# RMSNorm with repeated rows: row sums, roots and copies spread anew over the engines

## The chip, the cores and the metric

One core of a Trainium2 chip. The metric is the device time of one execution in microseconds, median over several.

## The reference

```python
def reference(x, gamma):                      # x: 8 x 512 x 2048, gamma: 2048, float32
    x_rep = np.repeat(x, 2, axis=1)
    rms = np.sqrt((x_rep ** 2).mean(axis=-1, keepdims=True) + 1e-6)
    return ((x_rep / rms) * gamma[None, None, :]).astype(np.float32)
```

Each row of x is divided by its root mean square, multiplied by gamma, and written twice: 33.6 MB are read and 67.1 MB written.

## The kernel before

The rows go through in eight tiles of 128 partitions by four rows, in three buffers of eight rows each. A load fills the upper four rows. The results are put in every second row and copied to the rows between, and one 8 MB store takes the whole buffer. All loads and stores are issued by SyncE into one queue.

```python
    def square(i, k):                          # ScalarE: one row's sum of squares, then its root
        sq = junk.tile([P, D], f32, name="sq")
        ss = small.tile([P, 1], f32, name="ss")
        nc.scalar.activation(out=sq[:], in_=ys[i][:, K * (R - 1) + k, :], func=Act.Square, accum_out=ss[:])
        rms = small.tile([P, 1], f32, name="rms")
        nc.scalar.activation(out=rms[:], in_=ss[:], func=Act.Sqrt, scale=inv_d, bias=eps_t[:])
        return rms

    def scale(i, k, rms):                      # VectorE: x * (1 / rms) * gamma, one row
        rstd = small.tile([P, 1], f32, name="rstd")
        nc.vector.reciprocal(out=rstd[:], in_=rms[:])
        nc.vector.scalar_tensor_tensor(...)

    def compute(i):
        for k in range(K):
            scale(i, k, square(i, k))
        repeat(i, 0, K // 2, nc.scalar.copy)
        repeat(i, K // 2, K, nc.vector.tensor_copy)

    load(0, nc.sync, parts=2)
    # ... seven pieces of gamma by ScalarE's queue into one partition ...
    nc.gpsimd.partition_broadcast(out_ap=gamma_b[:], in_ap=gamma_b[0:1, :])
    # ...
    loads_after = {2: (3, 4, 5), 4: (6, 7)}
    for i in range(ntiles):
        compute(i)
        store(i, 0, K)
        for j in loads_after.get(i, ()):
            load(j, nc.sync)
```

Of the kernel before, what the change touches and what calls it, by code (L numbers as in the profile page):

```python
# [1 line left out]

# [4 lines left out]


@with_exitstack
def kernel(  # L10
    ctx: ExitStack,
    tc: tile.TileContext,
    x: bass.AP,
    gamma: bass.AP,
    out: bass.AP,
):
    nc = tc.nc
    P = nc.NUM_PARTITIONS
    f32 = mybir.dt.float32
    Act = mybir.ActivationFunctionType  # L20
    Alu = mybir.AluOpType

    B, S, D = x.shape
    Bo, So, Do = out.shape
    R = So // S
    assert R == 2 and D == Do and B == Bo and So == S * R
    eps = 1e-6
    inv_d = 1.0 / float(D)


    K = 4
    N = B * S
    assert N % (P * K) == 0
    ntiles = N // (P * K)
    x_t = x.rearrange("b s d -> (b s) d").rearrange("(n p k) d -> n p k d", p=P, k=K)
    out_t = out.rearrange("b s d -> (b s) d").rearrange("(n p j) d -> n p (j d)", p=P, j=K * R)

    singles = ctx.enter_context(tc.tile_pool(name="singles", bufs=1))
    rows = ctx.enter_context(tc.tile_pool(name="rows", bufs=3))
    junk = ctx.enter_context(tc.tile_pool(name="junk", bufs=1, space=bass.MemoryType.PSUM))  # L40
    small = ctx.enter_context(tc.tile_pool(name="small", bufs=8))

    ys = []

    def load(i, eng, parts=1):


        y = rows.tile([P, K * R, D], f32, name="y")
        step = K // parts
        for k in range(0, K, step):  # L50
            at = K * (R - 1) + k
            eng.dma_start(out=y[:, at : at + step, :], in_=x_t[i, :, k : k + step, :])
        ys.append(y)

    def store(i, k0, k1):
        nc.sync.dma_start(  # L56
            out=out_t[i, :, R * k0 * D : R * k1 * D],
            in_=ys[i][:, R * k0 : R * k1, :].rearrange("p j d -> p (j d)"),
        )

    def square(i, k):
        sq = junk.tile([P, D], f32, name="sq")
        ss = small.tile([P, 1], f32, name="ss")
        nc.scalar.activation(  # L64
            out=sq[:], in_=ys[i][:, K * (R - 1) + k, :], func=Act.Square, accum_out=ss[:]
        )
        rms = small.tile([P, 1], f32, name="rms")
        nc.scalar.activation(out=rms[:], in_=ss[:], func=Act.Sqrt, scale=inv_d, bias=eps_t[:])  # L68
        return rms

    def scale(i, k, rms):
        rstd = small.tile([P, 1], f32, name="rstd")
        nc.vector.reciprocal(out=rstd[:], in_=rms[:])  # L73
        nc.vector.scalar_tensor_tensor(  # L74
            out=ys[i][:, R * k, :], in0=ys[i][:, K * (R - 1) + k, :], scalar=rstd[:], in1=gamma_b[:],
            op0=Alu.mult, op1=Alu.mult,
        )

    def repeat(i, k0, k1, copy):
        y_r = ys[i].rearrange("p (k r) d -> p k r d", r=R)  # L80
        copy(out=y_r[:, k0:k1, 1, :], in_=y_r[:, k0:k1, 0, :])  # L81

    def compute(i):
        for k in range(K):
            scale(i, k, square(i, k))
        repeat(i, 0, K // 2, nc.scalar.copy)
        repeat(i, K // 2, K, nc.vector.tensor_copy)


    ctx.enter_context(tc.manual_schedule())  # L90
    load(0, nc.sync, parts=2)
    gamma_b = singles.tile([P, D], f32, name="gamma_b")
    cuts = [0, *range(D // 4, D + 1, D // 8)]
    for c0, c1 in zip(cuts, cuts[1:]):
        nc.scalar.dma_start(out=gamma_b[0:1, c0:c1], in_=gamma[c0:c1].partition_broadcast(1))  # L95
    nc.gpsimd.partition_broadcast(out_ap=gamma_b[:], in_ap=gamma_b[0:1, :])  # L96
    eps_t = singles.tile([P, 1], f32, name="eps_t")
    nc.vector.memset(eps_t, eps)  # L98
    load(1, nc.sync)
    load(2, nc.sync)  # L100



    assert ntiles == 8
    loads_after = {2: (3, 4, 5), 4: (6, 7)}
    for i in range(ntiles):
        compute(i)
        store(i, 0, K)
        for j in loads_after.get(i, ()):
            load(j, nc.sync)  # L110


# [1 line left out]
_INS = ['x', 'gamma']  # L114
_OUTS = [((8, 1024, 2048), 'float32')]


# [23 lines left out]
```

## Time and profile before

| | before |
|---|---|
| time, median of 6 runs | 239.77 us (239.54 to 240.25) |
| span of the profiled run | 237.9 us |
| VectorE / ScalarE / GpSimd busy | 41% / 42% / 1% |
| share of the sync queue's packets | 98.5% of sixteen engines |

The time is some 2 us over the span (239.77 against 237.9). The prediction shows the lines that carry the bound. Two more groups of this kernel's page show what the change set out to remove. The columns are line, engine, operation, tiles and count, then busy us and mean ns, then the engine's idle time just before and what ended most of it. The third line is the only work that GpSimd does here, but for four fills of constants at the start (0.1 us each).

```profile
L73 DVE RECIPROCAL rstd<-rms 128x1 f32<-128x1 f32 x32 | 5.0, 158 | 94.6 <-ACT rms L68 94.3
...
L68 ACT ACTIVATE rms<-ss,eps_t 128x1 f32<-128x1 f32 x32 | 9.4, 295 | 1.0
...
L96 POOL PARTITION_BROADCAST gamma_b<-gamma_b x1 | 2.3, 2294 | 12.2 <-DMA y<-in_x_dram 12.2
```

Each row has a root on ScalarE and a reciprocal on VectorE, 32 of each, and VectorE's idle time is put down to the root. It idles mostly because the data isn't there yet (ScalarE, which makes the roots, itself waits 87.8 us for loads), not because a root takes 295 ns.

### The profile page before, as it was taken

To read this page: it belongs to the slowest core of one execution; us is meant where nothing else is said; L and a number is where in the kernel's file an instruction comes from. 1 tells how busy PE (TensorE), PEld (TensorE's weight loads), DVE (VectorE), ACT (ScalarE), POOL (GpSimd) and SP (SyncE) were. 2 spreads that over 40 slices of the span, in tenths; PEclk is the share of its full clock that TensorE was granted. 3 is DMA by queue.
4 is the path that set the end of the run, shared out by engine and by line. 5 is a ranking of instruction groups with operands and counts; after the bars stand their busy time and mean duration, and the time that the engine had idled before them with its cause. 6 is when DMAs were issued, how large, how long until landed. Compare 5 with 4: busy or idle time off the path is not lost.

```text
span 237.9 us, 287 instructions
## 1 busy us (share of the span) xinstructions
DVE 96.5 (41%) x73; ACT 101.0 (42%) x106; POOL 2.5 (1%) x5
## 2 busy tenths in 40 slices
DVE  0049999960000000059999960000199990000000
ACT  2697999900000000099999920000599960000000
POOL 0030000000000000000000000000000000000000
DMA  7999998989899998999998999989998989999994
GB/s 265 436 446 441 441 441 353 530 353 496 386 452 430 397 485 353 441 441 441 441 518 364 464 419 430 452 369 430 435 518 364 518 364 485 397 452 430 408 474 176
DMA packets 2464, 100.69 MB, mean 423 GB/s; under 512 B 279, under 2 KB 285, under 8 KB 286
## 3 DMA queue, kind: packets, MB, share of 16 engines
q1 hardware_dynamic: 2448, 100.66, 98.5%
q14 instruction: 2, 0.02, 0.0%
q10 hardware_dynamic: 14, 0.01, 0.0%
HBM read 33.56 MB, written 67.11 MB: 423 GB/s over the span
## 4 chain that ended last, share of the span: by engine, by line
DMA 58%; ACT 12%; DVE 9%; issue 1%; POOLq 1%; ACTq 1%; SPq 0%
DMA y<-in_x_dram 33%; DMA out_dram<-y 21%; ACT sq L64 8%; DVE y L74 7%; DMA gamma_b<-in_gamma_dram 4%; ACT y L81 3%; DVE y L81 2%; ACT rms L68 1%; POOLq L136 1%; ACTq L95 1%; DVE rstd L73 0%; POOLq L96 0%; SPq L56 0%
## 5 line engine op out<-in xcount | busy, mean ns | idle before, releaser
L64 ACT ACTIVATE sq<-y 128x2048 f32<-128x2048 f32 x32 | 59.7, 1865 | 87.8 <-DMA y<-in_x_dram 87.8
L74 DVE SCALAR_TENSOR_TENSOR y<-y,rstd,gamma_b 128x2048 f32<-128x2048 f32 x32 | 75.3, 2352 | 4.1 <-POOL gamma_b L96 3.0
L73 DVE RECIPROCAL rstd<-rms 128x1 f32<-128x1 f32 x32 | 5.0, 158 | 94.6 <-ACT rms L68 94.3
L81 ACT COPY y<-y 128x4096 f32<-128x4096 f32 x8 | 28.7, 3590 | 1.4 <-DVE y L74 1.4
L81 DVE COPY y<-y 128x4096 f32<-128x4096 f32 x8 | 18.3, 2294 | 0.3
L68 ACT ACTIVATE rms<-ss,eps_t 128x1 f32<-128x1 f32 x32 | 9.4, 295 | 1.0
L64 ACT ACTIVATION_READ_ACCUMULATOR sq<-y 128x1 f32 x32 | 6.0, 187 | 0.0
L64 ACT ACT_TABLE_LOAD x1 | 1.3, 1283 | 3.0 <-issue 3.0
L96 POOL PARTITION_BROADCAST gamma_b<-gamma_b x1 | 2.3, 2294 | 12.2 <-DMA y<-in_x_dram 12.2
L68 ACT ACT_TABLE_LOAD x1 | 1.3, 1283 | 0.0
L98 DVE MEMSET eps_t<- 128x1 f32 x1 | 0.1, 59 | 0.8 <-PEq L125 0.8
L125 POOL MEMSET const-uint8-127<- 128x1 uint8 x1 | 0.1, 102 | 0.0
L125 POOL MEMSET const-bfloat16-1.0<- 128x1 bf16 x1 | 0.1, 101 | 0.0
L125 POOL MEMSET const-float32-0.0<- 128x1 f32 x1 | 0.1, 98 | 0.2 <-issue 0.2
L125 POOL MEMSET const-float32-1.0<- 128x1 f32 x1 | 0.1, 98 | 0.0
## 6 DMA issues: line engine op xcount, KB each, us to landing
y<-in_x_dram SPq DMA_DIRECT2D x7, 4096.0 KB, 14.6
y<-in_x_dram SPq DMA_DIRECT2D x2, 2048.0 KB, 7.4
out_dram<-y SPq DMA_DIRECT2D x8, 24.4
gamma_b<-in_gamma_dram ACTq DMA_DIRECT2D x6, 1.0 KB
gamma_b<-in_gamma_dram ACTq DMA_DIRECT2D x1, 2.0 KB
```

The lines of the kernel that those rows point to most:

```text
L64: nc.scalar.activation(out=sq[:], in_=ys[i][:, K * (R - 1) + k, :], func=Act.Square, accum_out=ss[:])
L68: nc.scalar.activation(out=rms[:], in_=ss[:], func=Act.Sqrt, scale=inv_d, bias=eps_t[:])
L73: nc.vector.reciprocal(out=rstd[:], in_=rms[:])
L74: nc.vector.scalar_tensor_tensor(out=ys[i][:, R * k, :], in0=ys[i][:, K * (R - 1) + k, :], scalar=rstd[:], in1=gamma_b[:], op0=Alu.mult, o ...
L81: copy(out=y_r[:, k0:k1, 1, :], in_=y_r[:, k0:k1, 0, :])
L95: nc.scalar.dma_start(out=gamma_b[0:1, c0:c1], in_=gamma[c0:c1].partition_broadcast(1))
L96: nc.gpsimd.partition_broadcast(out_ap=gamma_b[:], in_ap=gamma_b[0:1, :])
L98: nc.vector.memset(eps_t, eps)
L125: nc = _bacc.Bacc("TRN2", target_bir_lowering=False, num_devices=1)
L136: with _tile.TileContext(nc) as tc:
```

## The change

Its intent: fewer and wider instructions, with each engine's work ordered so that none waits for another. Row sums are made of wide squares (ScalarE) and wide sums (VectorE), roots as a power -0.5 on GpSimd for a whole tile, tile 5's copy on GpSimd, and a tile's squares ahead of the former tile's copies. Gamma's pieces go into the sync queue. Cut to its core:

```diff
-    def square(i, k):
-        # ... one row: square with sum, then sqrt, both on ScalarE
+    def square(i, k0, k1):
+        nc.scalar.activation(
+            out=ys[i][:, k0:k1, :], in_=ys[i][:, x_at + k0 : x_at + k1, :], func=Act.Square
+        )
+    def reduce(i, k0, k1, ss):
+        nc.vector.tensor_reduce(
+            out=ss[:, k0:k1], in_=ys[i][:, k0:k1, :], op=Alu.add, axis=mybir.AxisListType.X
+        )
+    def root(k0, k1, ss):
+        at = ss[:, k0:k1]
+        nc.gpsimd.tensor_scalar(
+            out=at, in0=at, scalar1=inv_d, scalar2=eps, op0=Alu.mult, op1=Alu.add
+        )
+        nc.gpsimd.tensor_tensor(out=at, in0=at, in1=power_t[:, k0:k1], op=Alu.pow)
 # ... cut: gamma's pieces go to the sync queue, into two half rows ...
-    nc.gpsimd.partition_broadcast(out_ap=gamma_b[:], in_ap=gamma_b[0:1, :])
+    for c0 in (0, D // 2):
+        nc.gpsimd.partition_broadcast(out_ap=gamma_b[:, c0 : c0 + D // 2], in_ap=gamma_half(c0))
 # ... cut: by_rows() and mixed() order the parts of one tile ...
-    for i in range(ntiles):
-        compute(i)
-        store(i, 0, K)
+    by_rows(0, whole)
+    two = mixed(sums(1, 1), shared, ahead=(2, 1))
+    mixed(two, shared)
 # ... cut: loads 3, 4, 5 ...
+    by_rows(3, shared)
+    _, _, ss = mixed(sums(4, H), whole, ahead=(5, 0))
 # ... cut: loads 6, 7 ...
+    reduce(5, 0, K, ss)
+    root(0, K, ss)
+    # ... tile 5: four ScalarE copies with a scale, one VectorE multiply of 8192 by gamma ...
+    repeat(5, 0, K, nc.gpsimd.tensor_copy)
+    store(5)
+    last = mixed(sums(6, 1), by_scalar, ahead=(7, 0))
+    mixed(last, shared)
```

More of the change, by code (lines that the diff above doesn't have):

```diff
@@ L43, with new_tile, load @@
     ys = []
-    def load(i, eng, parts=1):
-        y = rows.tile([P, K * R, D], f32, name="y")
-        step = K // parts
-        for k in range(0, K, step):
-            at = K * (R - 1) + k
-            eng.dma_start(out=y[:, at : at + step, :], in_=x_t[i, :, k : k + step, :])
-        ys.append(y)
-    def store(i, k0, k1):
+    def new_tile():
+        ys.append(rows.tile([P, K * R, D], f32, name="y"))
+    def load(i, k0, k1):
         nc.sync.dma_start(
-            out=out_t[i, :, R * k0 * D : R * k1 * D],
-            in_=ys[i][:, R * k0 : R * k1, :].rearrange("p j d -> p (j d)"),
-        )
@@ L61, in square, with store, total @@
-    def square(i, k):
+            out=ys[i][:, K * (R - 1) + k0 : K * (R - 1) + k1, :], in_=x_t[i, :, k0:k1, :]
+        )
+    def store(i):
+        nc.sync.dma_start(out=out_t[i], in_=ys[i].rearrange("p j d -> p (j d)"))
+    H = K // 2
+    x_at = K * (R - 1)
+    def total(i, k, ss):
         sq = junk.tile([P, D], f32, name="sq")
-        ss = small.tile([P, 1], f32, name="ss")
         nc.scalar.activation(
-            out=sq[:], in_=ys[i][:, K * (R - 1) + k, :], func=Act.Square, accum_out=ss[:]
+            out=sq[:], in_=ys[i][:, x_at + k, :], func=Act.Square, accum_out=ss[:, k : k + 1]
@@ L66, in square @@
         )
-        rms = small.tile([P, 1], f32, name="rms")
-        nc.scalar.activation(out=rms[:], in_=ss[:], func=Act.Sqrt, scale=inv_d, bias=eps_t[:])
-        return rms
-    def scale(i, k, rms):
-        rstd = small.tile([P, 1], f32, name="rstd")
-        nc.vector.reciprocal(out=rstd[:], in_=rms[:])
-        nc.vector.scalar_tensor_tensor(
-            out=ys[i][:, R * k, :], in0=ys[i][:, K * (R - 1) + k, :], scalar=rstd[:], in1=gamma_b[:],
-            op0=Alu.mult, op1=Alu.mult,
-        )
@@ L79, in repeat @@
-    def repeat(i, k0, k1, copy):
+    def square(i, k0, k1):
+        nc.scalar.activation(
+            out=ys[i][:, k0:k1, :], in_=ys[i][:, x_at + k0 : x_at + k1, :], func=Act.Square
+        )
+    def reduce(i, k0, k1, ss):
[8 more added lines that the diff above has]
+        nc.gpsimd.tensor_tensor(out=at, in0=at, in1=power_t[:, k0:k1], op=Alu.pow)
@@ L80, in repeat, with scale, columns @@
+    def scale(i, k0, k1, rstd):
+        for k in range(k0, k1):
+            nc.vector.scalar_tensor_tensor(
+                out=ys[i][:, R * k, :], in0=ys[i][:, x_at + k, :], scalar=rstd[:, k : k + 1],
+                in1=gamma_b[:], op0=Alu.mult, op1=Alu.mult,
+            )
+    def repeat(i, k0, k1, copy=nc.scalar.copy):
         y_r = ys[i].rearrange("p (k r) d -> p k r d", r=R)
         copy(out=y_r[:, k0:k1, 1, :], in_=y_r[:, k0:k1, 0, :])
-    def compute(i):
-        for k in range(K):
-            scale(i, k, square(i, k))
-        repeat(i, 0, K // 2, nc.scalar.copy)
-        repeat(i, K // 2, K, nc.vector.tensor_copy)
+    def columns():
+        return small.tile([P, K], f32, name="ss")
@@ L90 @@
     ctx.enter_context(tc.manual_schedule())
-    load(0, nc.sync, parts=2)
+    assert ntiles == 8
     gamma_b = singles.tile([P, D], f32, name="gamma_b")
     cuts = [0, *range(D // 4, D + 1, D // 8)]
-    for c0, c1 in zip(cuts, cuts[1:]):
-        nc.scalar.dma_start(out=gamma_b[0:1, c0:c1], in_=gamma[c0:c1].partition_broadcast(1))
-    nc.gpsimd.partition_broadcast(out_ap=gamma_b[:], in_ap=gamma_b[0:1, :])
-    eps_t = singles.tile([P, 1], f32, name="eps_t")
-    nc.vector.memset(eps_t, eps)
@@ L99, with gamma_half, gamma_piece @@
-    load(1, nc.sync)
-    load(2, nc.sync)
-    assert ntiles == 8
-    loads_after = {2: (3, 4, 5), 4: (6, 7)}
-    for i in range(ntiles):
-        compute(i)
-        store(i, 0, K)
-        for j in loads_after.get(i, ()):
-            load(j, nc.sync)
+    for _ in range(3):
+        new_tile()
+    gamma_row = singles.tile([64, D // 2], f32, name="gamma_row")
+    def gamma_half(c):
+        at = 32 * (c // (D // 2))
+        return gamma_row[at : at + 1, :]
+    def gamma_piece(c0, c1):
+        at = c0 % (D // 2)
+        nc.sync.dma_start(
+            out=gamma_half(c0)[:, at : at + c1 - c0], in_=gamma[c0:c1].partition_broadcast(1)
+        )
@@ new lines @@
+    power_t = singles.tile([P, K], f32, name="power_t")
+    nc.gpsimd.memset(power_t, -0.5)
+    eps_t = singles.tile([P, 1], f32, name="eps_t")
+    nc.gpsimd.memset(eps_t, eps)
+    nc.scalar.preload_act_table(Act.Sqrt)
+    load(0, 0, H)
+    for c0, c1 in zip(cuts[:-2], cuts[1:-1]):
+        gamma_piece(c0, c1)
+    load(0, H, K)
+    gamma_piece(cuts[-2], cuts[-1])
+    for c0 in (0, D // 2):
+        nc.gpsimd.partition_broadcast(out_ap=gamma_b[:, c0 : c0 + D // 2], in_ap=gamma_half(c0))
@@ new lines, with root_quick, by_rows @@
+    load(1, 0, K)
+    load(2, 0, K)
+    def root_quick(k0, k1, ss):
+        at = ss[:, k0:k1]
+        nc.scalar.activation(out=at, in_=at, func=Act.Sqrt, scale=inv_d, bias=eps_t[:])
+        nc.vector.reciprocal(out=at, in_=at)
+    def by_rows(i, copies):
+        ss = [columns() for _ in range(R)]
+        for h, k0 in enumerate(range(0, K, H)):
+            for k in range(k0, k0 + H):
+                total(i, k, ss[h])
+            root_quick(k0, k0 + H, ss[h])
+            scale(i, k0, k0 + H, ss[h])
+        for k0, k1, copy in copies:
+            repeat(i, k0, k1, copy)
+        store(i)
@@ new lines, in sums, with mixed @@
+    def sums(i, by_row):
+        ss = columns()
+        square(i, by_row, K)
+        for k in range(by_row):
+            total(i, k, ss)
+        return i, by_row, ss
+    def mixed(given, copies, ahead=None):
+        i, by_row, ss = given
+        reduce(i, by_row, K, ss)
+        root(0, K, ss)
+        if ahead is not None:
+            ahead = sums(*ahead)
+        scale(i, 0, K, ss)
+        for k0, k1, copy in copies:
+            repeat(i, k0, k1, copy)
+        store(i)
+        return ahead
@@ new lines @@
+    whole = ((0, K, nc.vector.tensor_copy),)
+    shared = ((0, H, nc.scalar.copy), (H, K, nc.vector.tensor_copy))
+    by_scalar = ((0, H, nc.scalar.copy), (H, K, nc.scalar.copy))
+    by_rows(0, whole)
+    two = mixed(sums(1, 1), shared, ahead=(2, 1))
+    mixed(two, shared)
+    for j in (3, 4, 5):
+        new_tile()
+        load(j, 0, K)
+    by_rows(3, shared)
+    _, _, ss = mixed(sums(4, H), whole, ahead=(5, 0))
+    for j in (6, 7):
+        new_tile()
+        load(j, 0, K)
+    reduce(5, 0, K, ss)
@@ new lines @@
+    root(0, K, ss)
+    for k in range(K):
+        nc.scalar.activation(
+            out=ys[5][:, R * k, :], in_=ys[5][:, x_at + k, :], func=Act.Copy, scale=ss[:, k : k + 1]
+        )
+    y_r = ys[5].rearrange("p (k r) d -> p k r d", r=R)
+    nc.vector.tensor_tensor(
+        out=y_r[:, :, 0, :], in0=y_r[:, :, 0, :],
+        in1=gamma_b[:].rearrange("p (k d) -> p k d", k=1).to_broadcast([P, K, D]), op=Alu.mult,
+    )
+    repeat(5, 0, K, nc.gpsimd.tensor_copy)
+    store(5)
+    last = mixed(sums(6, 1), by_scalar, ahead=(7, 0))
```

## The prediction

> **What bounds the kernel now.** I read the page from the top: the busy shares, then the slices, then the queues.
>
> ```profile
> DVE 96.5 (41%) x73; ACT 101.0 (42%) x106; POOL 2.5 (1%) x5
> ...
> DVE  0049999960000000059999960000199990000000
> ACT  2697999900000000099999920000599960000000
> POOL 0030000000000000000000000000000000000000
> DMA  7999998989899998999998999989998989999994
> GB/s 265 436 446 441 441 441 353 530 353 496 386 452 430 397 485 353 441 441 441 441 518 364 464 419 430 452 369 430 435 518 364 518 364 485 397 452 430 408 474 176
> ...
> q1 hardware_dynamic: 2448, 100.66, 98.5%
> ...
> HBM read 33.56 MB, written 67.11 MB: 423 GB/s over the span
> ```
>
> No compute engine is busy for half of the span, and each has long empty stretches. The DMA row has none: the sync queue (q1) fills 98.5% of sixteen engines. So the time is 100.66 MB over what the engines move, plus a start and an end.
>
> Then the chain of waits in order of time, for how the queue is fed:
>
> ```profile
> 27.05 25.77 DMA out_dram<-y
> ...
> 52.84 48.32 DMA y<-in_x_dram
> ...
> 115.86 24.36 DMA out_dram<-y
> ...
> 140.24 29.08 DMA y<-in_x_dram
> ```
>
> The reader sees transfers that take 25 to 48 us, though a 4 MB load needs some 9.7 us and an 8 MB store 19.4 (stores 0, 1 and 2 landed at 52.84, 72.14 and 91.56 us by the loads that waited for them: 19.3 and 19.4 apart). They wait behind others in one queue. The order there is loads 0, 1, 2, stores 0, 1, 2, loads 3, 4, 5, stores 3, 4, loads 6, 7, stores 5, 6, 7, and the listing of the changed kernel's instructions by engine has the same order, but for the seven small gamma pieces, which move into it.
>
> So **the question is only whether every store is issued before the queue runs dry.** The trace's packet records give the deadlines. The packets of load 2 end on the first of the sixteen engines at 32.41 us, of store 0 at 51.73, store 1 at 71.05, load 5 at 119.41, store 3 at 138.73, load 7 at 177.41, store 5 at 196.73, store 6 at 216.05. The very first load was issued at 0.72 and its first packet began at 1.73, so a store has to be issued 1.0 us ahead: at 31.4, 50.7, 70.0, 118.4, 137.7, 176.4, 195.7 and 215.0 for stores 0 to 7. Before, they were issued at 27.05, about 39, 51.4, 115.9, 128.3, 160.1, 184.0 and 196.4: 2.5 to 19 us early.
>
> The costs of the parts, from the groups:
>
> ```profile
> L64 ACT ACTIVATE sq<-y 128x2048 f32<-128x2048 f32 x32 | 59.7, 1865 | 87.8 <-DMA y<-in_x_dram 87.8
> L74 DVE SCALAR_TENSOR_TENSOR y<-y,rstd,gamma_b 128x2048 f32<-128x2048 f32 x32 | 75.3, 2352 | 4.1 <-POOL gamma_b L96 3.0
> ...
> L81 ACT COPY y<-y 128x4096 f32<-128x4096 f32 x8 | 28.7, 3590 | 1.4 <-DVE y L74 1.4
> L81 DVE COPY y<-y 128x4096 f32<-128x4096 f32 x8 | 18.3, 2294 | 0.3
> ```
>
> [...]
>
> **The change, part by part.** *Gamma*: the pieces leave ACT's queue and go into the sync queue, broadcast in two halves. Before, the last landed at 12.4 and the broadcast ended at 14.9. Now the last piece sits behind load 0's second half (13.0), and half a broadcast (1.15, half of 2294 ns) ends at about 14.4. Worth half a us to the first scale, nothing to the queue.
> *Tile 0 and 3, by rows*: two square-sums (2.03 us start to start) before a root, in place of one. On tile 0 gamma decides: four scales of 2.39 start to start from 14.4, one reciprocal of 0.2, then one DVE copy of 8192 elements (estimate 4.43: twice 2294 less one fixed cost of 160 ns) end at 28.6.
> *Tiles 1, 2, 4, 6, 7*: wide squares on ACT[...], a wide sum on DVE[...], then the root on GpSimd, for which DVE waits. Call R the gap from the end of the sum to the first scale: two GpSimd instructions and three hand-overs. A GpSimd memset of one element took 0.10 us; with a power of unknown cost I choose R = 1.3, and would believe 0.7 to 2.5. DVE then gains 4.4 to 8.7 us of work a tile and has R idle, where before it waited 0.19 per row for a reciprocal.
>
> Issue times of the stores:
> Store 0: 28.6, deadline 31.4.
> Store 1: sum from 28.6 to 35.2, +R, four scales 9.6, copy 2.3: 47.1 + R = 48.4, deadline 50.7.
> Store 2: the same again after it, 18.5 + R: 65.6 + 2R = 68.2, deadline 70.0.
> Store 3: before, it was issued 14.7 after load 3 landed (101.15). The root now needs a second square-sum (+2.03), and two reciprocals drop out of the row of scales (2.46 a row before, 2.39 without): 117.8, deadline 118.4.
> Store 4: DVE is free at 117.8, sum 4.4, R, scales 9.6, copy of four rows 4.4: 136.4 + R = 137.7, deadline 137.7.
> Store 5: sum 8.7 and R after 136.3 + R, four ACT copies with a scale of 2.0, one DVE multiply over 8192 (8.7): 162 + 2R = 164.6, then the GpSimd copy of 8192, [...]deadline 176.4.
> Store 6: load 6 landed at 169.32; squares 5.3, sum 6.6, R, scales 9.6, then ACT's second copy 3.6: 194.5 + R = 195.8, deadline 195.7.
> Store 7: DVE goes on at 190.9 + R with 8.7, R, 9.6, 2.3: 211.5 + 2R = 214.1, deadline 215.0.
>
> So the engines have used up nearly all of the queue's slack, but hardly more. Lateness adds: once a store is late by x, all after it moves by x. At R = 1.3 the sum is 0.1 at store 6[...]; engines that end 0.5 us later than the first hide some of it. At R = 2.0: 0.65 + 0.8 = 1.45 us. At R = 3: 1.65 + 1.8 at stores 4 and 6, and 1.6 at store 2: 5 us.
>
> **The rivals.** (a) *Hidden anyway*: R is near 0.7[...]; every store is in time and the kernel keeps 240.0. For it speaks that the DMA row has no gap and that even now most deadlines hold on paper; against it, four margins of 0.6 us or less (stores 3, 4, 5, 6). (b) *The root takes the place of the waits removed*: a power on GpSimd costs 2 us or more, and DVE becomes the bound of stores 2, 4, 6 and 7. R = 2 gives 241.5, R = 3 gives 245. Nothing in this profile shows a GpSimd operation of that kind, which is what speaks for keeping it open. (c) *The GpSimd copy is late*: [...] Against it: only one tile is given to GpSimd, whose load lands some 56 us before its store is due. (d) *A gain at the start*, since the small packets no longer alternate with large ones on one engine: the records show all sixteen engines busy from about 2.5 us on, so at most 0.3 us.
>
> **Range and chances.** All data still passes one queue at the same rate, so the floor is where it was: 239.5 to 240.0. I put half of the weight on (a), a third on a mild form of (b) or (c), costing 0.5 to 3 us, and a tenth on a strong one. The middle is 240.5, the range 239.4 to 243.0. Faster by 2% would need under 235.3, which is below what the queue's 98.5% allows: 0.01. Slower by 2% is over 244.9, which needs R near 3 or a copy above 16 us: 0.10. Within 2%: 0.89.
>
> **What would show each step right or wrong.** The DMA row stays at 8 and 9 tenths and the queue's share at 97% or more, with DVE's busy time up from 96.5 to about 135 us (28 scales 65.9, six sums 41.5, copies 18.0, the multiply 8.7, reciprocals 0.6). The sync queue's issue times should be those above within 1 us; the groups should show the sum of 6144 at 6.5 us, the square at 5.3, the copy of 8192 at 4.4, and DVE's idle time before a scale put down to GpSimd, R each. I am wrong if R is above 2.5, if the GpSimd copy takes over 12 us, if the last gamma piece holds up load 1, or if the packets themselves run slower beside busier engines, which would show as a longer store spacing than 19.4 us.

The stores' times above use 5.3 us for a square and 6.6 for a sum of 6144, 4.4 for a sum of 4096, and 8.7 for a sum or a multiply of 8192. No run had shown these; the changed kernel's trace then had 5.32, 6.55, 4.42, 8.68 and 8.69. Store 5 came to 171.6 at the earliest and 176.9 at the latest, so at R = 1.3 perhaps 0.5 us late, beside the 0.1 at store 6; that is store 5's margin in (a), and (c) rested on it. The other estimates are from the page: the 160 ns taken off the copy of 8192 is what one reciprocal of 128x1 takes (158 ns), and half a broadcast was put at 1.15 us and later took 1.30. As to (d), the records of the kernel before have gamma's six packets of 1 KB (0.05 us each) 0.7 to 1.3 us apart; in the changed kernel five of them follow each other in 0.2 us.

## The result, and the profile after

| | before | after |
|---|---|---|
| time, median of 6 runs | 239.77 us (239.54 to 240.25) | 243.32 us (242.75 to 243.77) |
| ratio, 95% interval | | 1.0144 (1.0127 to 1.0162) |
| span of the profiled run | 237.9 us | 241.8 us |

A ratio is the mean time of one kernel's fast runs over that of the other's in the same rounds, so it is not quite the ratio of the medians. The changed kernel is 1.4% slower: within 2%, but 0.3 us beyond the predicted range. The page of the changed kernel: busy shares, the slices, the queue and the rate.

```profile
DVE 133.2 (55%) x45; ACT 90.8 (38%) x47; POOL 17.2 (7%) x21
...
POOL 0220001001000000000010001007401001000000
DMA  7999999898989899999999898979999898989890
GB/s 268 421 439 412 434 412 520 347 520 347 520 358 510 369 434 417 434 434 434 439 423 445 379 488 379 499 276 434 434 428 510 358 510 358 499 369 499 369 499 33
...
q1 hardware_dynamic: 2462, 100.67, 97.7%
HBM read 33.56 MB, written 67.11 MB: 416 GB/s over the span
```

VectorE is busier by 36.7 us, as intended, and still idle for 45% of the span. The same 100.7 MB move at 416 GB/s, where they moved at 423. Neighbouring slices swing between some 350 and 520, as whole rounds of packets fall into one or the other (sixteen packets of 64 KB are 1.05 MB, which is 176 GB/s over a slice of 6 us), so only what no neighbour makes up is a loss. Three slices stand out: the fourth (18 to 24 us) has 412 GB/s where the kernel before had 441, the 27th (157 to 163 us) has 276, and in the last only 33 are left, where the kernel before still moved 176. The loss is in several places. Then the groups, which answer the prediction's unknown costs:

```profile
L87 DVE SCALAR_TENSOR_TENSOR y<-y,ss,gamma_b 128x2048 f32<-128x2048 f32 x28 | 64.8, 2350 | 10.0 <-POOL ss L83 7.4
...
L197 DVE TENSOR_TENSOR y<-y,gamma_b 128x8192 f32<-128x8192 f32 x1 | 8.7, 8693 | 9.3 <-ACT y L193 9.3
L80 POOL TENSOR_SCALAR ss<-ss 128x4 f32<-128x4 f32 x6 | 1.2, 194 | 158.2 <-DVE ss L74 158.2
L94 POOL COPY y<-y 128x8192 f32<-128x8192 f32 x1 | 7.0, 7009 | 16.6 <-DVE y L197 16.6
L83 POOL TENSOR_TENSOR ss<-ss,power_t 128x4 f32<-128x4 f32 x6 | 6.1, 1016 | 0.5
```

The root costs 0.19 + 1.02 us on GpSimd, and VectorE waits 7.4 us for it in five tiles: R is about 1.5. The copy took 7.0 us. Neither is near what the prediction called too dear (R above 2.5, a copy over 12 us). And the timeline of both kernels where tile 3 begins (start, duration, instruction, and in brackets the idle time before it); first before, then after. "x2" on the queue's line is two issues in one entry, the second at its end.

```profile
101.18 1.88 ACT L64 ACTIVATE sq<-y 128x2048 f32<-128x2048 f32 x1 [53.03 <-DMA y<-in_x_dram]
...
115.86 12.72 SPq L56 DMA_DIRECT2D out_dram<-y  x2
```

```profile
102.30 1.88 ACT L63 ACTIVATE sq<-y 128x2048 f32<-128x2048 f32 x1 [36.95 <-DMA y<-in_x_dram]
...
118.76 19.97 SPq L56 DMA_DIRECT2D out_dram<-y  x2
...
124.60 9.26 DVE L87 SCALAR_TENSOR_TENSOR y<-y,ss,gamma_b 128x2048 f32<-128x2048 f32 x4 [1.48 <-POOL ss L83]
```

Tile 3 needs nothing but load 3, and **load 3 is seen 1.1 us later** than before, though no engine has yet been late for any store. From there stores 3 and 4 are issued at 118.76 and 138.39 us.

The packet records tell why. For each transfer they give the time at which each of the sixteen engines ended its last packet (us; "middle" is the median engine):

| transfer | before: middle, last | after: middle, last |
|---|---|---|
| load 1 | 22.06, 22.31 | 22.12, 23.66 |
| load 3 | 100.31, 100.69 | 99.98, 101.87 |
| load 5 | 119.74, 120.12 | 119.35, 121.23 |
| store 3 | 139.08, 139.75 | 139.09, 140.55 |
| store 4 | 158.43, 159.13 | 159.51, 160.11 |
| load 7 | 177.86, 178.81 | 179.88, 182.31 |
| store 7 | 235.84, 236.76 | 238.07, 240.27 |

(1) In load 1, between 20.0 and 21.8 us, six packets on four engines take 0.3 to 1.2 us longer than their usual 1.21. The landings at load 1 count the engines: twelve at 22.26 to 22.71 us, as before, and four at 23.58 to 23.98. (2) The four stay behind up to store 3, and tile 3 starts only when load 3's last engine has landed: twelve landed by 100.53 and four at 101.86 to 102.22. (3) Stores 3 and 4 begin 0.36 and 0.23 us after the engines that are ahead ran dry. (4) From 156 us on, whole rounds of packets are slow. The round at 156 us, the last packets of store 4, hits the twelve engines that had run dry and spares the four, and the group is gone: store 4 lands at 159.51 to 160.44 on all sixteen. The engine that ends last of all is one of the four, but its lag is mostly new: 0.6 us behind the middle at store 4, it had packets at 160 and 178 us that took 1.8 and 0.7 us too long.

Sums from the same records fit the 3.5 us between the two last ends (240.27 less 236.76). Packets over their usual time cost 2.76 us an engine after load 0, against 1.13 before: 1.6. The two late starts: 0.6. The last engine ends 2.2 us after the middle one, against 0.9: 1.3. Together 3.5. This says where the time is, not yet what put it there.

### The profile page after: what moved, and what is told of

Its sections match the earlier page's. It is cut to its first block, busy times and chain, and to the rows that moved or that the text cites. A ratio compares the mean times of both kernels' runs of the same rounds, so it can differ in the third digit from the quotient of the medians.

```text
span 241.8 us, 230 instructions
## 1 busy us (share of the span) xinstructions
DVE 133.2 (55%) x45; ACT 90.8 (38%) x47; POOL 17.2 (7%) x21
## 5 line engine op out<-in xcount | busy, mean ns | idle before, releaser
L87 DVE SCALAR_TENSOR_TENSOR y<-y,ss,gamma_b 128x2048 f32<-128x2048 f32 x28 | 64.8, 2350 | 10.0 <-POOL ss L83 7.4
L74 DVE TENSOR_REDUCE ss<-y 128x3 f32<-128x6144 f32 (+2 forms) x6 | 41.4, 6904 | 12.8 <-ACT y L69 12.8
L69 ACT ACTIVATE y<-y 128x6144 f32<-128x6144 f32 (+2 forms) x6 | 33.6, 5604 | 28.8 <-DMA y<-in_x_dram 28.8
L63 ACT ACTIVATE sq<-y 128x2048 f32<-128x2048 f32 x13 | 24.4, 1874 | 44.2 <-DMA y<-in_x_dram 44.1
L94 ACT COPY y<-y 128x4096 f32<-128x4096 f32 x6 | 21.6, 3605 | 29.4 <-DVE y L87 29.4
L94 DVE COPY y<-y 128x4096 f32<-128x4096 f32 (+1 forms) x6 | 18.0, 3004 | 0.2
L193 ACT ACTIVATE y<-y,ss 128x2048 f32<-128x2048 f32 x4 | 7.8, 1994 | 18.8 <-POOL ss L83 18.8
L197 DVE TENSOR_TENSOR y<-y,gamma_b 128x8192 f32<-128x8192 f32 x1 | 8.7, 8693 | 9.3 <-ACT y L193 9.3
L94 POOL COPY y<-y 128x8192 f32<-128x8192 f32 x1 | 7.0, 7009 | 16.6 <-DVE y L197 16.6
L83 POOL TENSOR_TENSOR ss<-ss,power_t 128x4 f32<-128x4 f32 x6 | 6.1, 1016 | 0.5
```

What stands on the lines that cost most here:

```text
L63: nc.scalar.activation(out=sq[:], in_=ys[i][:, x_at + k, :], func=Act.Square, accum_out=ss[:, k : k + 1])
L69: nc.scalar.activation(out=ys[i][:, k0:k1, :], in_=ys[i][:, x_at + k0 : x_at + k1, :], func=Act.Square)
L74: nc.vector.tensor_reduce(out=ss[:, k0:k1], in_=ys[i][:, k0:k1, :], op=Alu.add, axis=mybir.AxisListType.X)
L83: nc.gpsimd.tensor_tensor(out=at, in0=at, in1=power_t[:, k0:k1], op=Alu.pow)
L87: nc.vector.scalar_tensor_tensor(out=ys[i][:, R * k, :], in0=ys[i][:, x_at + k, :], scalar=rstd[:, k : k + 1], in1=gamma_b[:], op0=Alu.mul ...
L94: copy(out=y_r[:, k0:k1, 1, :], in_=y_r[:, k0:k1, 0, :])
```

## The experiments

Theories, as they were formed: **A**, gamma's pieces in the sync queue make the four engines late; **B**, tile 5's work on GpSimd disturbs the packets; **C**, going from the broadcast to the arithmetic on GpSimd has a cost of its own, and the packets of load 1 suffer under that; **D**, stores that are issued just ahead of the queue's end, or just behind, cost more than their lateness; **E**, the wide squares and sums slow the packets. Ratios are to the kernel before, of the same rounds, with the 95% interval.

### again

The changed kernel, without an edit. 

> The changed kernel once more, for a second trace. In the first trace the packets of the stores started within 0.4 us of the end of those before them, so little was lost by late stores; the loss sat in packets longer than their usual 0.61, 1.21 and 2.42 us (236.0 us of packets per engine against 234.2 before), at 20, 30, 87, 156, 160 and 177 us, and in how far the last of the sixteen engines lags (2.3 us at the end against 1.4). If slow packets belong to the program (a place in the schedule), they come at the same places again, within 1 us; if they are the chip's chance, the places differ and only the total of some 243.3 us stays.

Measured: 243.15 us. Four engines were behind at load 1 again, and slow packets stood at the same places (20, 30, 156 and 177 us; the round at 87 us did not come again). So what is seen is no accident of one trace.

### tile5_dve: tile 5 done as tile 4 is

```diff
-    reduce(5, 0, K, ss)
-    # ... root, ScalarE's scaled copies, the wide multiply, GpSimd's copy, store(5)
+    mixed((5, 0, ss), whole)
```

> The changed kernel with tile 5 done like tile 4 (four scales and one copy on DVE; no ACT copies with a scale, no wide multiply, no GpSimd copy). Its store is then due about 162 us in place of 172. Theory B: the slow packets at 156, 160 and 177 us go, 1.5 to 2.5 us faster, 241 to 242. Theory A: no change, 243.3.

Measured: 243.71 us, 1.0166 (1.0140 to 1.0191). Nothing came back: B falls.

### before_gamma: gamma's new path alone, in the kernel before

```diff
-        nc.scalar.dma_start(out=gamma_b[0:1, c0:c1], in_=gamma[c0:c1].partition_broadcast(1))
-    nc.gpsimd.partition_broadcast(out_ap=gamma_b[:], in_ap=gamma_b[0:1, :])
+        nc.sync.dma_start(out=gamma_half(c0)[:, at : at + c1 - c0], in_=...)   # order as in the changed kernel
+    for c0 in (0, D // 2):
+        nc.gpsimd.partition_broadcast(out_ap=gamma_b[:, c0 : c0 + D // 2], in_ap=gamma_half(c0))
```

> The kernel before with gamma's pieces in the sync queue and two half broadcasts, nothing else. Theory A: 1 to 2 us slower than before, 241 to 242. Theory B: 239.8, as before.

Measured: 239.82 us, 1.0005 (0.9986 to 1.0025). A falls: the small pieces in the large queue cost nothing.

### gamma_act: gamma's old path in the changed kernel

```diff
-    nc.sync.dma_start(out=gamma_half(c0)[:, at : at + c1 - c0], in_=...)
+    nc.scalar.dma_start(out=gamma_b[0:1, c0:c1], in_=gamma[c0:c1].partition_broadcast(1))
```

> The changed kernel with gamma's seven pieces back on ACT's queue and one broadcast. Theory A (gamma's small packets in the sync queue hold up engines early, and four engines lag by 1.3 us from load 1 on): 1 to 2 us faster than the changed kernel, 241.5 to 242.3, no lagging group at load 1. Theory B (the loss comes from the late store 5 and the wide work about 148 to 177 us): no change, 243.3.

Measured: 246.46 us, 1.0280 (1.0261 to 1.0300). A failed experiment: the second half of load 0 was issued at 8.53 us in place of 3.01, and all that followed was 2.9 us later. Its time tells nothing for or against A. Its landings do: with gamma's pieces on their old path, load 1 still landed on twelve engines at 25.21 to 25.51 us and on four at 26.00 to 26.35, so the pieces don't make that group.

### root_act: the roots taken off GpSimd

From tile5_dve, with an 800-element fill after each root so that VectorE would wait about as long:

```diff
-        nc.gpsimd.tensor_scalar(out=at, in0=at, scalar1=inv_d, scalar2=eps, op0=Alu.mult, op1=Alu.add)
-        nc.gpsimd.tensor_tensor(out=at, in0=at, in1=power_t[:, k0:k1], op=Alu.pow)
+        nc.scalar.activation(out=at, in_=at, func=Act.Sqrt, scale=inv_d, bias=eps_t[:])
+        nc.vector.reciprocal(out=at, in_=at)
+        nc.vector.memset(pad_t[:, 0:800], 0.0)
```

> The run tile5_dve with its roots taken from GpSimd: a square root on ACT and a reciprocal on DVE, and a small fill of 800 elements on DVE so that the gap between sum and first scale stays near 1.5 us and the stores are issued when they were. GpSimd then does nothing after gamma's broadcast. Theory C (GpSimd, between the broadcast and its first arithmetic, changes what it runs; that and its later work slow four of the sixteen engines at 19.5 to 21.5 us, and the lag costs more at every turn between loads and stores): 240 to 241, no group of four engines behind at load 1. Theory D (stores issued 0.3 to 10 us ahead of their turn in place of 3 to 20 make the turns slow): no change, 243.7. Theory E (wide squares written to the buffers and wide sums slow the packets): no change, 243.7.

Measured: 241.02 us, 1.0059 (1.0040 to 1.0077). Load 1's last engine ended at 22.31, as in the kernel before, and 2.7 us of tile5_dve's 243.71 were gone. But stores 3 and 4 were issued 1.4 and 1.6 us earlier than in the changed kernel (117.36, 136.83), so C and D could both claim that.

### before_pow: one root on GpSimd, in the kernel before

Behind the broadcast, on a scratch tile that nothing reads:

```diff
     nc.gpsimd.partition_broadcast(out_ap=gamma_b[:], in_ap=gamma_b[0:1, :])
+    nc.gpsimd.tensor_scalar(out=probe_t[:], in0=probe_t[:], scalar1=inv_d, scalar2=eps, op0=Alu.mult, op1=Alu.add)
+    nc.gpsimd.tensor_tensor(out=probe_t[:], in0=probe_t[:], in1=power_t[:], op=Alu.pow)
```

> The kernel before with one multiply-add and one power of 128x4 on GpSimd after gamma's broadcast, on a scratch tile that nobody waits for. Theory C: a group of four engines behind by 1 to 1.5 us at load 1 or 2 and 1 to 3.5 us slower, 240.5 to 243. Theories D and E: 239.6.

Measured: 242.26 us, 1.0104 (1.0085 to 1.0123): **2.6 us for two instructions that take 2.1 us on an idle engine and that nothing waits for.** Load 1's last engine ended at 23.30. GpSimd's timeline of this kernel:

```profile
13.14 2.30 POOL L96 PARTITION_BROADCAST gamma_b<-gamma_b  x1 [12.71 <-DMA y<-in_x_dram]
26.52 1.08 POOL L101 TENSOR_SCALAR probe_t<-probe_t 128x4 f32<-128x4 f32 x1 [11.07 <-issue]
27.68 1.06 POOL L104 TENSOR_TENSOR probe_t<-probe_t,power_t 128x4 f32<-128x4 f32 x1
```

The reader sees 11.07 us between the broadcast and the first arithmetic, in which GpSimd waits for nothing that the profile shows ("issue"). The trace has MODIFY_POOL_CONFIG records on GpSimd: a pair at about 1 us in all seventeen traces, and a second pair right behind the broadcast in the five where arithmetic follows it (at 15.36 us here, at 15.01 in the changed kernel). These five are also the ones in which four engines land load 1 late. The slow packets of the changed kernel's load 1 (20.0 to 21.8 us) come between that pair and its first arithmetic (36.13), so the arithmetic itself can't have slowed them. What GpSimd does in the gap, and what these records stand for, no run shows. In this kernel the lag stays to the end: the last store landed on nine engines by 236.56 us and on the other seven at 237.53 to 239.10, where the kernel before ended at 237.11.

### before_pow_pe: the same arithmetic, but no broadcast on GpSimd

Gamma is spread over the partitions by TensorE (a row of ones times gamma), in the kernel before with the same two GpSimd instructions:

```diff
-    nc.gpsimd.partition_broadcast(out_ap=gamma_b[:], in_ap=gamma_b[0:1, :])
+    for c in range(0, D, 512):
+        nc.tensor.matmul(gamma_ps[:, c : c + 512], ones_t[:], gamma_b[0:1, c : c + 512], start=True, stop=True)
+    nc.vector.tensor_copy(out=gamma_b[:], in_=gamma_ps[:])
+    nc.gpsimd.tensor_scalar(out=probe_t[:], ...)      # and the power, as in before_pow
```

C is now two theories: in C1 the cost comes with the change from the broadcast to the arithmetic, in C2 with the arithmetic itself. This expectation and those of after_pe and after_pe2 called that change an exchange.

> The kernel before with the multiply-add and the power of 128x4 on GpSimd as in the run before_pow, but gamma spread by TensorE and a DVE copy[...]. Theory C1: 239.6, as before. Theory C2: 242.3, as before_pow.

Measured: 239.64 us, 1.0006 (0.9991 to 1.0022). The timeline of GpSimd:

```profile
1.08 0.19 POOL L111 TENSOR_SCALAR probe_t<-probe_t 128x4 f32<-128x4 f32 x1 [0.66 <-DVE eps_t L101]
1.36 1.02 POOL L114 TENSOR_TENSOR probe_t<-probe_t,power_t 128x4 f32<-128x4 f32 x1
```

The arithmetic runs at once, with no gap, and load 1's last engine ended at 22.22. The arithmetic alone costs nothing, and the kernel before has the broadcast alone; the two together cost 2.6 us. So much is shown. That the cost lies in the change from one to the other, which is C1, is inferred from the gap and the second pair of records; what the change consists of is not shown.

### after_pe: the same in the changed kernel, first try

```diff
-        nc.gpsimd.partition_broadcast(out_ap=gamma_b[:, c0 : c0 + D // 2], in_ap=gamma_half(c0))
+        for c in range(0, D // 2, 512):
+            nc.tensor.matmul(gamma_ps[:, c0 + c : c0 + c + 512], ones_t[at : at + 1, :], ...)
+        nc.vector.tensor_copy(out=gamma_b[:, c0 : c0 + D // 2], in_=gamma_ps[:, c0 : c0 + D // 2])
```

> The changed kernel with gamma spread over the partitions by TensorE (a column of ones times the row, then DVE copies from PSUM), so that GpSimd runs arithmetic only and never a broadcast; roots, tile 5 and all store times as in the changed kernel. Theory C1[...]: 240.5 to 241.5, no group of four engines behind at load 1; what is left is theory D's. Theory C2 (the arithmetic itself slows the transfers): 243.3.

Measured: 242.05 us, 1.0129 (1.0090 to 1.0168). A miss of the experiment: two matmuls and a copy behind the last piece of gamma were slower than half a broadcast, and store 0 was issued at 32.19, after the queue had run dry. All the same, no four engines were behind at load 1 (its last landing was at 22.69), as C1 has it.

### after_pe2: the same, with little behind the last piece of gamma

```diff
+    for c0, c1 in ((0, 512), (512, 1024), (1024, 1536), (1536, 1792), (1792, 2048)):
+        nc.tensor.matmul(gamma_ps[:, c0:c1], ones_t[at : at + 1, :], gamma_row[...], start=True, stop=True)
+        if c1 in (1792, 2048):
+            nc.vector.tensor_copy(out=gamma_b[:, done:c1], in_=gamma_ps[:, done:c1])
+            done = c1
```

> The run after_pe with gamma ready at some 14.5 us in place of 18.1 (only its last 256 columns wait for the last piece), so that store 0 is issued at about 29 us as in the changed kernel and not at 32.2, where the queue had already run dry. [...]everything else is the changed kernel. If the exchange costs here what it costs the kernel before (2.6 us): 240.6. If it and the late stores share part of their cost: 241 to 242. If it costs nothing here: 243.3.

Measured: 239.50 us (239.30 to 240.29), 1.0009 (0.9989 to 1.0030). **All of the 3.6 us is gone**, more than any of the three cases expected, with every wide square, wide sum and GpSimd root of the change in place, and with store 0 issued later than in the changed kernel (29.72 against 29.09). The page's rate and the timeline at tile 3:

```profile
GB/s 265 440 444 441 441 441 519 364 419 463 364 519 353 530 353 425 425 430 408 430 530 353 530 353 530 353 425 414 419 508 353 530 353 463 421 386 497 353 530 177
...
q1 hardware_dynamic: 2462, 100.67, 98.6%
```

```profile
100.43 1.88 ACT L64 ACTIVATE sq<-y 128x2048 f32<-128x2048 f32 x1 [34.92 <-DMA y<-in_x_dram]
...
116.88 19.98 SPq L57 DMA_DIRECT2D out_dram<-y  x2
```

The fourth slice is back at 441 and the last at 177. Load 3 is seen at 100.43 in place of 102.30, and store 3 is issued 16.45 us after that, as in the changed kernel (16.46). Of the 1.9 us some 1.6 are the lagging engines (load 3's last packet ended 0.3 us after the middle engine's, in place of 1.9); the middle engine too ended load 3 earlier, by 0.3 (99.68), since this run had no slow round in load 2.

### both_undone: the wide work, without GpSimd's arithmetic

root_act without its fill, and tile 3 row by row as before:

```diff
-    by_rows(3, shared)
+    for k in range(K):
+        total(3, k, ss3)
+        root_quick(k, k + 1, ss3)
+        scale(3, k, k + 1, ss3)
```

> The run root_act without its fill and with tile 3 row by row as before: no GpSimd arithmetic, and stores 3, 4 and 6 issued 2 to 4 us ahead of their turn; wide squares, wide sums and work ahead stay in six tiles. Theories C and D together: 239.6 to 240.2. Theory E (wide squares and sums cost): 240.7 to 241.2, as root_act or little less.

Measured: 239.39 us, 0.9995 (0.9978 to 1.0011). The wide squares and sums of six tiles cost nothing: E falls.

### before_late, before_margin, late_012, late_34, late_67: what late stores cost by themselves

The kernel before, with VectorE fills of a scratch tile ahead of its copy, chosen tile by tile so that the stores come later. No GpSimd arithmetic, so nothing follows the broadcast there:

```diff
+    PADS = [1900, 7500, 6900, 2700, 6900, 20000, 13500, 5400]   # before_late; elements to fill, by tile
+    # before_margin [1900, 6700, 6200, 700, 6900, 20000, 8500, 5400]
+    # late_012 [1900, 7500, 6900, 0, 0, 0, 0, 0]; late_34 [0, 0, 0, 3300, 6900, 0, 0, 0]; late_67 [0, 0, 0, 0, 0, 0, 11000, 5400]
         repeat(i, 0, K // 2, nc.scalar.copy)
+        left = PADS[i]
+        while left > 0:
+            nc.vector.memset(pad_t[:, 0 : min(left, D)], 0.0)
+            left -= D
         repeat(i, K // 2, K, nc.vector.tensor_copy)
```

All stores at about the changed kernel's times. 

> The kernel before with fills of a PSUM tile on DVE ahead of its copies, so that its stores are issued at 29, 49, 69, 119, 138, 172, 198 and 216 us as in the changed kernel; no wide work, no root on GpSimd. Theory D: slow packets at 156 and 177 us as in the changed kernel and 2 to 3.5 us slower, 241.5 to 243. Theories C and E: 239.6, at most 0.5 more for the small gaps before stores 3, 4 and 6.

Measured: 241.58 us, 1.0093 (1.0061 to 1.0125). D holds in part. In its trace store 6 was issued at 198.77, after the queue had run dry, a gap of about 1 us.

All stores 2 to 4 us ahead. 

> The run before_late with smaller fills: stores 3, 4, 6 and 7 issued 2 to 4 us ahead of their turn in place of 0.2 to 0.9 late or ahead. Theory D in its sharp form (only a store issued within about 1 us of its turn slows the transfers around it): 239.6 to 240.1. If every delay of a store costs, however early it still is: 240.5 to 241.5.

Measured: 240.73 us (239.53 to 241.44), 1.0047 (1.0012 to 1.0082). Scattered, so inconclusive. The trace kept is of the run of 240.94 us: two engines landed the last store at 238.3, the other fourteen by 236.8.

Only stores 0 to 2. 

> The kernel before with fills ahead of the copies of tiles 0, 1 and 2 alone: stores 0 to 2 issued at 29, 49 and 69 us, 1.3 to 3.5 us ahead of their turn; the rest early as before. Theory D sharp (about 1 us decides): 239.4 to 239.9. If any lateness of a store costs: 240 to 241.

Measured: 239.5, 239.63, 240.27 and 241.37 us, 1.0028 (0.9994 to 1.0061). Mostly nothing, with one run of four that isn't explained. The trace kept is of that run (241.37): fifteen engines landed the last store by 236.8 us, much as in the kernel before, and one at 238.76.

Only stores 3 and 4. 

> The kernel before with fills in tiles 3 and 4 alone: stores 3 and 4 issued at about 118.7 and 138.4 us, 0.6 us or less ahead of their turn, as in the changed kernel. Theory D sharp: the packets at 156 us become slow and the kernel takes 240.3 to 241.2. If the slow packets at 156 us come from elsewhere: 239.6.

Measured: 241.64 us (241.53 to 241.81), 1.0089 (1.0074 to 1.0104). They were issued at 119.31 and 138.97, and their first packets began at 120.15 and 139.81, where in the kernel before they began at 119.41 and 138.73. The sixteen engines stood idle for 0.45 us on the mean before store 3 and 0.25 before store 4. The price was 2.0 us over the kernel before of that round (239.57), 0.4 more than D expected at most. The page's rate:

```profile
GB/s 263 438 437 437 437 437 350 526 350 525 350 525 350 525 350 437 437 432 426 366 526 350 525 350 525 350 350 437 437 350 525 350 525 350 525 350 525 350 525 175
```

The 20th slice (114 to 120 us) drops to 366 where the queue runs dry, though the next, with 526, makes most of that up, and at the 26th and 27th (150 to 162 us) 350 stands twice in a row, with no 525 to make it up. The fourth is at 437 and the last at 175: no engine lags here, so this is D without C. The packet records have the slow rounds at 156 and 177 us: 0.77 us an engine in store 4 and 0.87 in load 7. The account of the profiled run: 0.7 us idle and 1.8 us more of slow packets than in the kernel before, less 0.6, since the last engine ended only 0.3 us after the middle one and not 0.9.

Only stores 6 and 7. 

> The kernel before with fills in tiles 6 and 7 alone: store 6 issued about 0.5 us ahead of its turn, store 7 about 2. Theory D sharp: 0.2 to 0.5 us, 239.8 to 240.2, and the packets at 177 us stay as quick as before, since nothing ahead of them is late.

Measured: 239.64 us, 1.0008 (0.9993 to 1.0023). Nothing, with store 6 issued 1.2 us ahead of the queue's end.

The packet records of all seventeen traces then show a step. "Lead" is how long before the middle engine's last packet of the transfer ahead a store was issued; from an issue to its first packet it took 1.01 us at load 0 of the kernel before and 0.84 at stores 3 and 4 of late_34. "Excess" is the packets' time over the usual, in us an engine.

| kernels | lead of stores 3, 4 | excess in store 4 | in all, after load 0 |
|---|---|---|---|
| after, again, tile5_dve, gamma_act, before_late, late_34 | 0.28 to 1.18 | 0.57 to 0.77 | 2.5 to 3.5 |
| root_act, after_pe, after_pe2 | 1.78 to 2.16 | 0.08 to 0.18 | 1.0 to 2.1 |
| before and the other seven | 2.92 to 11.8 | at most 0.09 | 1.1 to 1.9 |

Where stores 3 and 4 were late or nearly so, slow packets follow at 156 us, some 17 us after store 4. after_pe has the like earlier: stores 0 to 2 met a dry queue there, and the last packets of store 2 were slow (0.83 us an engine, at 89 us). Slow packets at 177 us are a weaker sign: root_act, after_pe and after_pe2 have 0.5 to 0.8 us of them too. late_34 shows that the lateness brings those at 156 us; by what mechanism, no run tells.

## Why the prediction was wrong

**Where it was right.** The steps on the engines hold. The square of 6144 was to take 5.3 us and took 5.32; the sum 6.5 and took 6.55; the copy of 8192 on VectorE 4.43 and took 4.43; on GpSimd it took 7.0, which brings store 5 to the 171.6 of its early case. VectorE's busy time was put at 135 and is 133.2. R was chosen as 1.3 and is 1.48. Stores 0 to 5 were issued at 29.1, 49.2, 68.7, 118.8, 138.4 and 172.0 us, each within 1.0 of its predicted time. Stores 6 and 7 were 2.6 and 2.3 late (198.37, 216.36), behind a load 6 that landed 2.7 later than before (171.97 against 169.32). Rival (b), a dear root, and rival (c), a late copy, fell by these; (d) had no sign of it. One of its sums is off: store 4's parts (117.8, 4.4, 9.6 and 4.4) come to 136.2 + R and not 136.4, which gives 0.2 us of margin in place of none.

**Where it failed.** The failed step is "All data still passes one queue at the same rate, so the floor is where it was". The packets did not pass at the same rate: in load 1 four of sixteen engines fell 1.3 us behind, after the broadcast and before the first arithmetic (20.0 to 21.8 us, between 15.10 and 36.13). The prediction took the broadcast over from the kernel before and added arithmetic to the same engine, priced each by its own duration, and did not price the change from one to the other. Its own warning, packets that "run slower beside busier engines", came true, but not beside an engine that was busy: before_pow lost 2.6 us with GpSimd's added work at 2.1 us.

**The second term that was mis-sized** is the assumption "once a store is late by x, all after it moves by x", which no trace had shown. The margins it found were real: stores 3 and 4 had 0.6 and 0.0 us by its own sums (0.2 for store 4, redone). It took load 3's landing of 101.15 as given, which became 102.2, so the two stores came 1.0 and 0.7 later than it said. They cost 0.6 us of dry queue, and then more: late_34 pays 2.0 us, where its engines stood idle for 0.7.

**The chain, then.** In the changed kernel having arithmetic behind the broadcast makes four engines late (shown by before_pow against before_pow_pe: load 1's last engine ended at 23.30 and at 22.22), by what path is not shown. Load 3 counts as landed with its last engine (102.22, and tile 3 starts at 102.30), so it is seen 1.1 us later while twelve engines are on time. Tile 3's own work, 1.8 us longer than before (16.46 from the landing to the store, against 14.68), leaves no room for that, so stores 3 and 4 reach the queue as it runs dry, which brings slow packets later (late_34: 0.77 us an engine at 156 us). The four's lag itself ends in store 4, where the others become as late; in the kernel before, with before_pow, it stays to the end. Without the broadcast on GpSimd, neither the lag nor the dry queue appears (after_pe2: load 3's last packet ended 0.3 us after the middle engine's, and stores 3 and 4 had leads of 1.78 us or more).

**What stays open.** Why packets some 17 us after a nearly late store are slow; why single engines fall 2 us behind in before_margin and late_012; which four engines lag (the records kept don't number them), what GpSimd does between the broadcast and the arithmetic, and by which path that slows them: no run had the arithmetic ahead of the broadcast, or the pair at another time. Slow rounds at 30, 87, 117 or 176 us also appear in kernels that are fast (0.9 us in load 2 of the kernel before), so they are not by themselves a sign of harm. The split of the 3.6 us between lag and late stores isn't exact either: before_pow gives 2.6 for arithmetic behind a broadcast and late_34 2.0 for the stores, and these don't add: in the changed kernel the four's lag ends in store 4.

No variant was faster than the kernel before. The two best forms of the changed kernel, both_undone (0.9995) and after_pe2 (1.0009), stand at its time, with the queue as full (98.6% in both pages, against 98.5%).

## What to carry to other kernels

When a change puts a new kind of work on GpSimd, ask what else runs there: here arithmetic behind a broadcast cost the kernel before 2.6 us, though nothing waited for it, and four DMA engines were late. In a kernel bound by one queue, compute each store's lead over the end of the queue, keep some 2 us of it (here 1.8 and more left at most 0.2 us of slow packets in store 4), and look at the last engine's landing and not at the mean rate. Take the suspected neighbour away with the work kept in place, as after_pe2 does with the broadcast, before blaming the work.
